# Two value projections as seven quarter products each, with a quarter of both beside the preparation of x

## The chip, the core and the metric

The kernel runs on one core of a Trainium2 chip. Its engines work side by side, each through its own list of instructions in a fixed order: TensorE (PE: matrix products and transposes), VectorE (DVE), ScalarE (ACT), GpSimd (POOL) and SyncE (SP), which here issues nearly all transfers (DMAs) between HBM and the on-chip memory SBUF. TensorE writes into banks of PSUM, from which ACT and DVE read. An instruction that waits holds back all behind it on its engine. The metric is device time in microseconds; lower is better.

## The reference

One layer of a streaming encoder: an input projection, two attentions, two output projections. The change touches the input projection.

```python
def project(x, norm_w, w_in, q_norm_w, k_norm_w):
    h = rms_norm(x, norm_w) @ w_in
    sb_q, sb_k, sb_v, sb_z, cb_q, cb_k, cb_v, cb_z, g_sb, g_cb = jnp.split(h, SPLIT_POINTS, axis=-1)
    ...
```

x has 1024 prompt rows and 64 sample rows of 1024 elements; w_in has 6144 columns in float32. The values of the two branches are the 512 columns from 1024 (sb_v) and the 512 from 3072 (cb_v). cb_k and cb_q (from 2560 and 2048) are normalised per head. The values go out as results and are used by the attentions.

## The kernel before, in words

**Precision.** Every float32 operand is split into a high and a low half (a rounded copy, made by ACT, and the rest, made by a subtraction on DVE or POOL). A product is three matmuls: high by high, low by high, high by low. `whi`/`wlo` and `whix`/`wlox` are the halves of weights with 512 of the 1024 inner rows and 256 columns; x stands as `xa`, `xm`, `xb` (high and low halves of its two inner halves) with 1088 columns, one per token; `xs` holds the 64 sample rows, high beside low.

**First stage (L279 to L315, loop at L543).** Each of nine tiles of x (128 rows; the sample is tile 8) is squared and summed on ACT, its inverse root made on POOL, scaled on DVE (`xn`), turned by eight transposes into two PSUM tiles `pt`, and copied out by ACT and DVE. Beside this runs the first of six *natural* blocks of 256 columns: per token tile 24 matmuls of 128x256 (16 for the sample), 208 in a block. The blocks are sb_v's first half, cb_k, cb_k, cb_q, cb_q, sb_v's second half. A tile's result is in one of three PSUM banks (`acc`). For values, ACT copies it to `vst` (three buffers), which SP stores twice (L334 to L336). For q and k, `evac_nat` squares it on ACT, multiplies and sums on DVE, roots on POOL; `norm_nat` scales on ACT one tile later; `post_nat`, up to three tiles later, turns it through the one PSUM buffer `pk` and copies the halves to `hl`, which is stored for the attention.

**Sums.** `make_t` gives sixteen jobs: sums of x's four quarters (inner half by token half), t0 to t3, 544 columns each. A job is three additions on DVE (L189), a rounded copy on ACT (`t2h`, `t3h`, L172) and a rest on DVE (`t2l`, `t3l`, L173), put one job later. Half of the jobs run in the natural blocks (t0, t1); the eight for t2 and t3 begin at the fifth tile of the last block, into space that the work on q and k has left.

**Quarter products (L670 to L735).** cb_v is made by a scheme that needs seven products of quarters in place of eight: x quarters, their sums t0 to t3, and sums of weight quarters, combined by additions out of PSUM. Each has 48 matmuls (L706) with 256 weight columns; there are seven, with 32 sample matmuls (L656). Their weights are split by `split_quad` (L476 ACT, L478 POOL or DVE: eight splits, six on POOL). Then the next stage (L870) makes the remaining columns by the same scheme, using x, t0 to t3 and raw weights loaded by `load_raw`.

**What sets the order.** The program is written out in the order in which each engine performs it; there is no scheduler. SP performs loads and stores in the order of the code, and a load into a buffer waits until its last reader is done. On POOL there are only roots, splits and a few copies.

## Time and profile before

| | us |
|---|---|
| median of 3 runs | 958.56 (957.79 to 960.04) |
| the profiled execution | 960.42 |
| its span, first to last instruction | 958.6 |
| TensorE busy | 949.6 |
| DVE busy | 586.1 |
| ACT busy | 498.1 |
| POOL busy | 394.2 |
| first product (L530) starts | 9.65 |
| second natural block starts | 41.67 |
| first sample matmul of cb_v (L656) starts | 174.05 |
| next stage (L870) starts | 216.38 |

A row of a timeline is start, duration, engine, line, operation, output<-input, shape and count, and in brackets the engine's idle time before it and what ended that. Matmuls overlap: 0.28 us is one's latency, and the distance of starts is its pace. A row of DMAs gives the line's count, the size and the median time from issue to landing.

### The profile page before, as it was taken

The page shows a single profiled execution, that of the slowest core. Times are in us where ns is not written, and L with a number is a line of the kernel's source. Part 1 is how long each engine was busy: PE and PEld are TensorE (multiplying, and loading weights), DVE is VectorE, ACT ScalarE, POOL GpSimd, SP SyncE. Part 2 cuts the span into 40 slices and gives each one's busy share as a digit, 9 for nine tenths or more (in the row PEclk, how much of TensorE's full clock was granted, in tenths as well). Part 3 has the DMA queues.
Part 4 walks back from the last instruction along what each step waited for, and adds up shares of the span by engine and source line. Part 5 has one row for each costly group of instructions (what it writes and reads, how often), then busy time and mean ns, then how long its engine had stood idle before and what let it go on. Part 6 is the DMA issues. An engine that isn't in the chain of part 4 may idle for free.

```text
span 958.6 us, 20550 instructions
## 1 busy us (share of the span) xinstructions
PE 949.6 (99%) x7595; PEld 902.7 (94%) x7595; DVE 586.1 (61%) x1156; ACT 498.1 (52%) x1159; POOL 394.2 (41%) x393
## 2 busy tenths in 40 slices
PE   9999999999999999999999999999999999999998
PEld 8999999999999999999999988888888888999998
DVE  6656675974445555533322389777777775499735
ACT  6557774323434433333332476767886873466220
POOL 3276664244444666555532100111430012676641
PEclk9999999999999999999999999999999999999999
DMA  7747757145656555565424997768899933852742
GB/s 228 248 138 239 262 203 236 40 127 165 192 176 194 164 176 167 160 183 179 143 86 121 279 251 193 192 192 235 247 285 248 246 91 120 252 168 71 225 140 73
DMA packets 173497, 175.77 MB, mean 183 GB/s; under 512 B 30921, under 2 KB 157645, under 8 KB 173270
## 3 DMA queue, kind: packets, MB, share of 16 engines
...
## 4 chain that ended last, share of the span: by engine, by line
PE 92%; DVE 3%; ACT 2%; DMA 1%; POOL 1%; issue 1%; ACTq 0%; DVEq 0%
PE b L870 29%; PE acc L530 15%; PE o L1392 7%; PE z L1295 7%; PE pt L1348 7%; PE b L1717 6%; PE acc L1146 5%; PE acc L1039 5%; PE b L1188 4%; PE b L706 4%; PE pk L372 1%; PE pt L303 1%; DMA wraw<-in_w_in_dram 1%; DVE acc L1233 1%; PE acc L1760 1%
## 5 line engine op out<-in xcount | busy, mean ns | idle before, releaser
L1348 PE MATMUL pt<-ident,be 128*128 128x128 f32 (+1 forms) x568 | 87.1, 277 | 0.9 <-ACT wT L1357 0.6
L1295 PE MATMUL z<-ks,sq 128*128 128x320 f32 (+5 forms) x384 | 87.7, 338 | 0.0
L1317 DVE TENSOR_TENSOR_SCAN be<-be,imp 128x128 f32<-128x128 f32 (+7 forms) x64 | 82.8, 1342 | 8.1 <-ACT be L1298 8.0
L1357 ACT ACTIVATE wT<-pt 128x512 f32<-128x512 f32 (+3 forms) x123 | 57.2, 499 | 44.2 <-PE pt L1348 44.1
L1348 PEld LDWEIGHTS pt<-ident,be 128*128 128x128 f32 (+1 forms) x568 | 66.2, 140 | 13.7 <-issue 5.3
L870 PE MATMUL b<-xm,wlox 128*128 128x256 f32 (+1 forms) x336 | 76.0, 286 | 0.0
L878 DVE TENSOR_TENSOR u<-b,s 128x256 f32<-128x256 f32 (+1 forms) x56 | 24.3, 440 | 77.1 <-PE b L870 70.0
L1295 PEld LDWEIGHTS z<-ks,sq 128*128 128x128 f32 x384 | 63.5, 190 | 2.2 <-ACT be L1298 0.9
L1392 PE MATMUL o<-wT,vp 128*64 128x256 f32 (+1 forms) x608 | 64.1, 356 | 0.0
L1392 PEld LDWEIGHTS o<-wT,vp 128*64 128x64 f32 x608 | 40.3, 136 | 22.4 <-issue 5.4
L870 PEld LDWEIGHTS b<-xm,wlox 128*128 128x128 f32 x336 | 56.8, 188 | 0.0
L1320 ACT ACTIVATE be<-be,sm 128x640 f32<-128x640 f32 (+5 forms) x68 | 47.2, 694 | 17.7 <-DVE sm L1319 17.5
L530 PE MATMUL acc<-whi,xa 128*128 128x256 f32 x192 | 52.6, 294 | 0.0
...
L459 POOL TENSOR_TENSOR whix<-ws,whix 128x512 fp32r<-128x512 f32 x28 | 36.6, 1307 | 33.2 <-ACT whix L458 25.8
L1298 ACT ACTIVATE be<-z 128x384 f32<-128x384 f32 (+6 forms) x104 | 48.2, 521 | 3.1 <-PE z L1295 2.6
L530 PE MATMUL acc<-whi,xm 128*128 128x256 f32 x192 | 49.7, 278 | 0.0
L530 PE MATMUL acc<-wlo,xa 128*128 128x256 f32 x192 | 49.6, 278 | 0.0
L530 PE MATMUL acc<-whix,xb 128*128 128x256 f32 x192 | 49.6, 278 | 0.0
L530 PE MATMUL acc<-whix,xm 128*128 128x256 f32 x192 | 49.6, 278 | 0.0
L530 PE MATMUL acc<-wlox,xm 128*128 128x256 f32 x192 | 49.5, 278 | 0.0
L1308 ACT ACTIVATE be<-be,sm 128x640 f32<-128x640 f32 (+5 forms) x68 | 47.3, 695 | 3.8 <-DVE sm L1300 3.3
...
## 6 DMA issues: line engine op xcount, KB each, us to landing
wraw<-in_w_in_dram SPq DMA_DIRECT2D x31, 512.0 KB, 4.5
wrawx<-in_w_in_dram SPq DMA_DIRECT2D x16, 512.0 KB, 6.0
...
xt<-in_x_prompt_dram SPq DMA_DIRECT2D x8, 512.0 KB
d_kcbT<-hl SPq DMA_DIRECT2D x8, 512.0 KB, 6.0
d_qcbT<-hl SPq DMA_DIRECT2D x8, 512.0 KB, 4.3
ks<-d_ksbT SPq DMA_DIRECT2D x16, 256.0 KB, 4.6
```

What stands on the lines that cost most here:

```text
L530: TE.matmul(ps, x, w, start=first, stop=last)
L870: TE.matmul(ps[:, :m], w[:, hl_, k], right[s](x)[:, k, a:b], start=s < 3 and k == 0 and e == 0, stop=k == 3 and e == 2, skip_group_check=s ...
L1039: TE.matmul(ps[:, :b - a], w[:, k], xk(x, k)[:, a:b], start=k == 0 and n == 0, stop=k == KT - 1 and n == 2)
L1146: TE.matmul(ps[:, :e - a], w[:, p, cw], g[:, a:e], start=m % 12 == 0, stop=m % 12 == 11)
L1295: TE.matmul(z[:, :m], s[:, e, q0:q0 + 128], ks[:, h, o + x:o + y], start=(e, h) == parts[0], stop=(e, h) == parts[-1])
L1298: A.activation(be[:r, x:y], z[:r, :m], AF.Sigmoid, scale=-0.125)
L1308: A.activation(be[:, :n], be[:, :n], AF.Exp, bias=kp[:, j:j + 1], scale=-1.0, accum_out=kp[:, 2:3])
L1317: V.tensor_tensor_scan(be[:r, n - 1::-1], be[:r, n - 1::-1], im[:, ::-1], 0.0, op0=OP.mult, op1=OP.max)
L1348: TE.transpose(pt[:kr, x, :r], be[:r, kb * 128:kb * 128 + kr], ident[:r, :r])
L1357: A.activation(w[:, sl:sl + m, q0:q0 + r], pt[:, :m, :r], AF.Copy)
L1392: TE.matmul(o[hd * 64:hd * 64 + 64, c0:c1], vv[:kr, kb, hd * 64:hd * 64 + 64], wT[b, p, j, hd, s // 4][:kr, s % 4, c0:c1] if j < 4 else wT ...
L1717: TE.matmul(ps[:, t], left[s](xs_, k)[:, ts_], wt_[:, k], start=s < 3 and t == k == e == 0, stop=k == 3 and e == 2, skip_group_check=s > 2 ...
```

## The change

Both value projections are now made by the quarter scheme. For j=0 (sb_v) and j=1 (cb_v) the first two of the products (x's two inner halves of the first 512 tokens by the weights of the first 256 columns) need no sums: they are made beside the preparation of x, in place of the first natural block. The result of the first is copied to `vst` and stored to a new HBM buffer `d_s1`; the second goes on in the same PSUM bank and gives the final values. With them go the sample's products for these columns. These are 112 matmuls for each j (L552).

Then come four natural blocks (cb_k, cb_k, cb_q, cb_q; 832 matmuls), and the remaining ten quarter products in the order ORDER (480 matmuls, L783), with 32 for the sample's other columns (L686, the entries with s=0). `load_s1` loads the stored partial results into `u2` when the first quarter product is done; the first two products of j=0 are held in PSUM until then. t2's space is opened when the last q tiles are through, t3's when `hl` is; the sums for t2 and t3 are at the eight places of TJ. All twelve splits are on POOL (L496).

The columns of x are laid out anew: each half has 512 prompt and 32 sample columns, so that the sums and the next stage's output cut at even places (four transposes fewer; `pieces`, `out`). Tiles of x are prepared in the order 0, 1, 2, 3, 8, 4, 5, 6, 7. In the listings below, line numbers of the changed kernel lie 2 to 50 higher for the same code (L552 for L530, L336 for L334, L286 for L284, L174 for L172, L494 and L496 for L476 and L478).

First place: tiles 1 and 2 in the first stage on TensorE, before (`acc_324` is tile 0, `acc_387` tile 1, `acc_447` tile 2):

```order
L530 MATMUL acc_324<-wlo_274,xa_150 128x256 x4
L303 MATMUL pt_349<-ident_138,xn_305 128x128 x4
L303 MATMUL pt_356<-ident_138,xn_305 128x128 x4
L530 MATMUL acc_324<-wlox_276,xm_151 128x256 x4
L530 MATMUL acc_387<-whi_269,xa_150 128x256 x4
L530 MATMUL acc_387<-whix_272,xm_151 128x256 x4
L530 MATMUL acc_387<-whi_269,xm_151 128x256 x4
L530 MATMUL acc_387<-whix_272,xb_152 128x256 x4
L530 MATMUL acc_387<-wlo_274,xa_150 128x256 x2
```

and now (`acc_293` is tile 0, `acc_356` tile 1):

```order
L552 MATMUL acc_293<-wlox_283,xm_153 128x256 x4
L552 MATMUL acc_356<-whi_250,xa_152 128x256 x4
L552 MATMUL acc_356<-whi_250,xm_153 128x256 x4
L552 MATMUL acc_356<-wlo_259,xa_152 128x256 x4
L552 MATMUL acc_356<-whix_281,xm_153 128x256 x4
L552 MATMUL acc_356<-whix_281,xb_154 128x256 x2
L305 MATMUL pt_378<-ident_140,xn_337 128x128 x4
L305 MATMUL pt_385<-ident_140,xn_337 128x128 x4
```

A tile's 24 matmuls were one accumulation in any order; now the twelve with `whi`, `wlo` come first and are read out between, and the twelve with `whix`, `wlox` follow in the same bank.

ACT there, before (two tiles' copies out, `vst_383` and `vst_437`):

```order
L284 ACTIVATE sq_366,ms_367<-xt_205 128x1024
L320 ACTIVATE fl_378<-acc_280 64x256
L334 ACTIVATE vst_383<-acc_324 128x256
L313 ACTIVATE xa_150<-pt_406 128x4x128
L313 ACTIVATE xm_151<-pt_413 128x4x128
L284 ACTIVATE sq_423,ms_424<-xt_278 128x1024
L334 ACTIVATE vst_437<-acc_387 128x256
```

and now:

```order
L311 ACTIVATE xm_153<-pt_324 128x4x128
L286 ACTIVATE sq_331,ms_332<-xt_203 128x1024
L286 ACTIVATE sq_340,ms_341<-xt_208 128x1024
L336 ACTIVATE vst_352<-acc_293 128x256
L336 ACTIVATE vst_369<-acc_356 128x256
L311 ACTIVATE xa_152<-pt_378 128x4x128
L311 ACTIVATE xm_153<-pt_385 128x4x128
L286 ACTIVATE sq_395,ms_396<-xt_285 64x1024
L336 ACTIVATE vst_409<-acc_356 128x256
L133 ACTIVATE whi_418<-wraw_210 128x1024
L336 ACTIVATE vst_430<-acc_413 128x256
```

Each tile's bank is now read out twice, and squares and a weight split stand between the readings.

Second place: ACT in the quarter products, before (`whi_3054` is the last split but one):

```order
L476 ACTIVATE whi_2850<-s1_2759 128x1024
L476 ACTIVATE whix_2854<-wrawx_2404 128x1024
L711 ACTIVATE s1_2892<-b10_2867 128x512
L172 ACTIVATE t3h_2650<-d_2838 128x544
L711 ACTIVATE s1_2925<-b11_2900 128x512
L172 ACTIVATE t3h_2650<-d_2894 128x544
L476 ACTIVATE whi_2933<-wraw_2562 128x1024
L476 ACTIVATE whix_2991<-wraw_2243 128x1024
L172 ACTIVATE t3h_2650<-d_2927 128x544
L172 ACTIVATE t3h_2650<-d_3020 128x544
L476 ACTIVATE whi_3054<-q11_2564 128x1024
```

and now (`whi_2763`, `whix_2843`, `whi_2912`, `whi_3006` and `whix_3067` are for q=4, 5, 6, 8 and 9):

```order
L494 ACTIVATE whi_2763<-made2_2201 128x1024
L174 ACTIVATE t2h_2652<-d_2738 128x544
L174 ACTIVATE t2h_2652<-d_2787 128x544
L494 ACTIVATE whix_2843<-made1_2200 128x1024
L174 ACTIVATE t2h_2652<-d_2837 128x544
L174 ACTIVATE t3h_2699<-d_2874 128x544
L494 ACTIVATE whi_2912<-wrawx_2767 128x1024
L174 ACTIVATE t3h_2699<-d_2906 128x544
L494 ACTIVATE whix_2950<-wraw_2664 128x1024
L174 ACTIVATE t3h_2699<-d_2944 128x544
L174 ACTIVATE t3h_2699<-d_2983 128x544
L494 ACTIVATE whi_3006<-wrawx_2916 128x1024
```

All copies of the t2 and t3 sums but one now stand among the splits from q=4 on.

Third place: SP around the start of the quarter products, before:

```order
L335 DMA d_sbv_59<-vst_2799 128x256
L336 DMA out_3_dram<-vst_2799 128x256
L335 DMA d_sbv_59<-vst_2834 128x256
L336 DMA out_3_dram<-vst_2834 128x256
L412 DMA wraw_3058<-in_w_in_dram 128x4x256
L412 DMA wraw_3060<-in_w_in_dram 128x4x256
```

and now (`hl_2569` holds the last four tiles of q, `u200` and `u201` are `u2` of j=0):

```order
L487 DMA wrawx_2597<-in_w_in_dram 128x4x256
L53 DMA d_qcbT2_68<-hl_2569 256x1x512
L53 DMA d_qcbT3_69<-hl_2569 256x1x512
L487 DMA wraw_2664<-in_w_in_dram 128x4x256
L707 DMA u200_2707<-d_s10_126 128x512
L707 DMA u201_2708<-d_s10_126 128x512
```

Before, these were the stores of the last value block, with q stored earlier; now the last stores of q stand here, and the loads of the partial results behind them.

The diff, cut to its core:

```diff
-XO = 576
+XO = HF
+SW = 576
...
+    d_s1 = [dram.tile([128, 1024], F32, name=f"d_s1{j}") for j in range(2)]
...
-        NB = [1024, 2560, 2816, 2048, 2304, 1280]
-        NV = 3072
+        QO = [0, 1, 2, 3, 8, 4, 5, 6, 7]
+        NB = [1024, 3072, 2560, 2816, 2048, 2304]
...
+        def evac_v(i, t, ps, n):
+
+            if t == 8:
+                put_s(i, 0, fold(p0.tile([64, 256], F32, name="fl", bufs=1), ps))
+                return
+            v = p0.tile([128, 256], F32, name="vst", bufs=3)
+            A.activation(v, ps, AF.Copy)
+            if n == 0:
+                SP.dma_start(d_s1[i][:, 256 * t:256 * t + 256], v)
+                return
+            SP.dma_start(VD[i][0][128 * t:128 * t + 128, 0:256], v)
+            if i == 0:
+                SP.dma_start(o_sbv_p[128 * t:128 * t + 128, 0:256], v)
...
+        def early(at):
+            if at in READY:
+                ready(READY.index(at) + 1)
+            elif at == 52:
+                W.split((1, 0))
+            elif at == 88:
+                W.split((1, 1))
+                load_nat(2, 1)
+            elif at == 70:
+                SP.dma_start(wqk[:, 0], q_norm_w[0:1, :].to_broadcast([128, 64]))
+                SP.dma_start(wqk[:, 1], k_norm_w[0:1, :].to_broadcast([128, 64]))
+            elif at == 140:
+                load_rb()
+            elif at == 160:
+                W.split((2, 0))
+                load_nat(3, 0)
+            elif at == 196:
+                W.split((2, 1), V)
+                load_nat(3, 1)
+
...
+        READY = [20, 42, 62, 82, 106, 130, 154, 178]
+        at, opened, got = 0, {}, []
+        for i, todo in enumerate(([(t, n) for t in range(4) for n in (0, 1)] + [(8, 2)],
+                                  [(0, 0), (1, 0), (0, 1), (2, 0), (1, 1), (3, 0), (2, 1), (8, 2), (3, 1)])):
+            for t, h in todo:
+                if h != 1:
+                    opened[t] = (psA if len(got) % 3 == 2 else psF).tile([128, 512], F32, name="acc")[:, :256]
+                    got.append(t)
+                ps = opened[t]
+                if t == 8:
+                    steps = [(k, n) for n in range(2) for k in range(KT)]
+                else:
+                    steps = [(4 * h + k, n) for n in range(3) for k in range(4)]
+                for m, (k, n) in enumerate(steps):
+                    early(at)
+                    at += 1
+                    product(ps, t, 2 if t == 8 else 3, k, n, m == 0 and h != 1, m == len(steps) - 1)
+                evac_v(i, t, ps, h)
...
-                        W.split((i + 1, h), V if i == 0 and h else None)
-                    if i + 2 < nb:
-                        load_nat(i + 2, h)
-                    elif i + 2 == nb:
-                        load_quad(h, 0, *((natx, "wrawx", 1) if h else (wpool, "wraw", 2)))
-                if (i, ti) == (0, 4):
-                    load_rb()
+                        W.split((i + 1, h))
+                        if i + 2 < nb:
+                            load_nat(i + 2, h)
+                        elif h == 0:
+                            load_quad(0, 1, 1)
+                        else:
+                            load_quad(0, 0, 1)
+                            load_quad(0, 0, 0, True)
+                    elif h == 0:
+                        split_quad(made[2])
+                        load_quad(0, 1, 0, True)
+                        load_quad(1, 1, 1)
+                    else:
+                        split_quad(made[1])
...
+                if (i, ti) == (nb - 1, 1):
+                    for n in (1, 2):
+                        made[n] = pn.tile([128, 4, 256], F32, name=f"made{n}", bufs=1)
+                    sum_w(1, quad[0, 0, 1], quad[0, 1, 1], OP.add)
+                if (i, ti) == (nb - 1, 2):
+                    sum_w(2, made[1], quad[0, 0, 0], OP.subtract)
...
+        LEFT = {1: sum_of(1), 2: sum_of(0), 6: half_of(1, 1), 4: sum_of(2), 5: sum_of(3)}
+        ORDER = [(0, 1), (0, 2), (0, 6), (0, 0), (1, 1), (1, 2), (1, 6), (1, 0), (0, 4), (0, 5), (1, 4), (1, 5)]
+        SPLIT = {(0, 1): (0, 1, 0), (1, 0): (0, 0, 1), (2, 1): 2, (4, 0): 1, (5, 0): (1, 1, 0), (5, 2): (1, 0, 1),
+                 (6, 1): (0, 0, 0), (8, 0): (0, 1, 1), (9, 0): (1, 0, 0), (10, 0): (1, 1, 1)}
+        LOAD = {(0, 1): [(1, 0, 0, True)], (1, 0): [(1, 0, 1)], (2, 1): [(1, 1, 0, True), (0, 0, 1)],
+                (5, 0): [(0, 0, 0, True)], (5, 2): [(1, 0, 0)], (6, 0): [(1, 0, 1)], (6, 1): [(0, 1, 1, True)],
+                (8, 0): [(1, 1, 1, True)]}
+        TJ = [(1, 1), (2, 0), (2, 2), (4, 0), (4, 2), (5, 0), (5, 2), (6, 0)]
+        BANKS = {0: "2", 2: "1", 4: "3", 5: "2", 6: "1", 8: "3", 10: "2"}
+        u, bank, held = {}, {}, []
+
+        def load_s1(j, pool):
+            for x in "23":
+                u[j, x] = [pool.tile([128, 512], F32, name=f"u{x}{j}{c}", bufs=1) for c in range(2)]
+            for c in range(2):
+                SP.dma_start(u[j, "2"][c], d_s1[j][:, 512 * c:512 * c + 512])
+
+        def evac_p(j, s, c, ps):
+            if s < 3:
+                d = u[j, "23"[s - 1]][c]
+                V.tensor_tensor(out=d, in0=ps, in1=u[j, "2"][c], op=OP.add)
+                return
+            v = nu.tile([128, 512], F32, name="o")
+            V.tensor_tensor(out=v, in0=ps, in1=u[j, "2" if s == 5 else "3"][c], op=OP.add)
+            put_v(j, 0 if s == 6 else 1, 0 if s == 5 else 1, c, v)
...
+        for q, (j, s) in enumerate(ORDER):
             if s == 0:
+                sample(j, 0, comb[3 + 4 * j])
+                continue
+            wh, wl = comb[q]
             for c in range(2):
                 for tt in range(2):
+                    at = q, 2 * c + tt
+                    if q == 0:
+                        if at == (0, 0):
+                            norm_nat(*raw1)
+                            pend.append(raw1[:3])
+                            sum_w((0, 1, 0), quad[0, 1, 0], made[2], OP.subtract)
+                        post_nat(*pend.pop(0))
+                    elif at == (1, 0):
+                        assert not pend
+                        p1x.close()
+                        open_t((2,))
+                        pst.close()
+                        psB = sx.enter_context(tc.tile_pool(name="a2p", bufs=1, space=PS))
+                    elif at == (1, 2):
+                        p1hx.close()
+                        open_t((3,))
+                        nu = ph.enter_context(tc.tile_pool(name="nu", bufs=2))
+                        nux = ExitStack()
+                        load_s1(0, nux.enter_context(tc.tile_pool(name="nua", bufs=1)))
+                    elif at == (2, 1):
+                        sum_w(1, quad[1, 0, 1], quad[1, 1, 1], OP.add)
+                        sum_w(2, made[1], quad[1, 0, 0], OP.subtract)
+                    elif at == (4, 0):
+                        load_s1(1, nu)
+                    elif at == (4, 1):
+                        sum_w((1, 1, 0), quad[1, 1, 0], made[2], OP.subtract)
+                    elif at == (6, 0):
+                        sum_w((0, 0, 0), quad[0, 0, 0], quad[0, 0, 1], OP.subtract)
+                    elif at == (8, 0):
+                        sum_w((1, 0, 0), quad[1, 0, 0], quad[1, 0, 1], OP.subtract)
+                    elif at == (10, 0):
+                        nux.close()
+                    elif at == (10, 2):
+                        prep(0)
+                    elif at == (11, 0):
+                        ws = sx.enter_context(tc.tile_pool(name="ws", bufs=3, side="right"))
+                        presum(1)
+                        prep(1)
+                    if at in TJ:
+                        next(tjobs)
+                    if at == (2, 0):
+                        for e in held:
+                            evac_p(*e)
+                    if at in SPLIT:
+                        n = SPLIT[at]
+                        split_quad((made if isinstance(n, int) else quad)[n])
+                    for e in LOAD.get(at, ()):
+                        load_quad(*e)
+                    if at == (9, 0):
+                        load_raw(0)
+                        load_raw(1)
+                    elif at == (10, 0):
+                        load_raw(2)
+                    if tt == 0 and s != 5:
+                        bank[c] = psF.tile([128, 512], F32, name="acc") if q == 1 else bank_of(BANKS[q], c)
+                    o = bank[c][:, 256 * tt:256 * tt + 256]
                     for k in range(4):
                         for e, (xe, w) in enumerate(((0, wh), (1, wh), (0, wl))):
+                            TE.matmul(o, LEFT[s](xe, k, 2 * c + tt), w[:, k], start=s != 5 and k == e == tt == 0,
                                       stop=k == 3 and e == 2, skip_group_check=True)
+                if q < 2:
+                    held.append((j, s, c, bank[c]))
+                else:
+                    evac_p(j, s, c, bank[c])
+            if s == 5:
+                sample(j, 1, comb[q])
         assert not list(tjobs)
```

328 lines of the change are left out of this document (105 added, 223 removed).

## The prediction

> **What bounds the kernel now.** I read the page first (busy shares, chain), then TensorE's waits, then the timelines of the first 44 us and of 155 to 216 us, where the change works.
>
> ```profile
> span 958.6 us, 20550 instructions
> PE 949.6 (99%) x7595; PEld 902.7 (94%) x7595; DVE 586.1 (61%) x1156; ACT 498.1 (52%) x1159; POOL 394.2 (41%) x393
> PE 92%; DVE 3%; ACT 2%; DMA 1%; POOL 1%; issue 1%; ACTq 0%; DVEq 0%
> ```
> ```profile
> PE pc L486 <- POOL half L257: 1.4, 1, 1.4
> ...
> PE acc L656 <- POOL wlo L478: 0.3, 1, 0.3
> ```
>
> TensorE is busy for 99% of the span and makes up 92% of the chain of waits; of the rows of what TensorE waited for (total, times, longest), the first is its longest wait and the last the only one between 155 and 216 us. So two things count: how many matmuls there are, and every wait that the new order puts before one.
>
> **Fewer matmuls.** The pace, from TensorE's timeline (start, duration), 16 matmuls apart:
>
> ```profile
> 41.67 0.28 PE L530 MATMUL acc<-whi,xs 128*128 128x256 f32 x1
> ...
> 43.48 0.28 PE L530 MATMUL acc<-whi,xa 128*128 128x256 f32 x1
> ```
>
> That is 1.81/16 = 0.113 us each. Before there are 6x208 natural products, 336 of quarters and 32 of samples: 1616. After there are 224 early ones, 4x208, 480 and 32: 1568. The 48 fewer are worth 5.4 us. Output transposes fall from 44 to 40; eight took 0.79 us (first and last row here), so 0.4. The 0.3 us wait above goes too. Gain: 6.1 us, all on the path. It is the only gain.
>
> **The early products (the 224 beside x's preparation).** They end before at 43.48 (16 of them lie in the second block). TensorE, ACT and POOL there:
>
> ```profile
> 9.65 1.03 PE L530 MATMUL acc<-whi,xs 128*128 128x256 f32 x4
> 25.64 1.04 PE L303 MATMUL pt<-ident,xn 128*128 128x128 f32 x8
> 26.43 0.48 PE L530 MATMUL acc<-whi,xm 128*128 128x256 f32 x2
> ```
> ```profile
> 10.01 1.05 ACT L131 ACTIVATE whix<-wrawx 128x1024 fp32r<-128x1024 f32 x1
> 11.64 0.60 ACT L313 ACTIVATE xm<-pt 128x512 fp32r<-128x512 f32 x1
> 12.12 1.06 ACT L284 ACTIVATE sq<-xt 128x1024 f32<-128x1024 f32 x1
> 13.30 1.06 ACT L284 ACTIVATE sq<-xt 128x1024 f32<-128x1024 f32 x1
> 18.52 0.38 ACT L334 ACTIVATE vst<-acc 128x256 f32<-128x256 f32 x1
> ```
>
> Without a stall: 9.65 + 224x0.113 + eight groups of transposes at 0.79 = 41.3, so before stalls some 2 us here. After, each tile's second product (t,1) goes on in the bank of its first, and its first matmul waits until ACT has copied (t,0) out. TensorE has 12 matmuls (1.36 us) of cover, and ACT works through other things first. For tile 1 these are two copies of x (0.5 each from row to row), two squares (1.15 each with their read-back), the copy of (0,1) and the copy of (1,0) (0.38 each): 4.1 us from about 13.2, so 17.3, where TensorE has finished (1,0) at 15.6: 1.7 us. The same count gives 0.65 for tile 0 (whix stands ahead), 1.65 for tile 2 (the whole split of the next weights, 1.05, stands ahead), 1.7 for tile 3, 0.6 for the sample; and the three vst buffers, each held by a store (4.1 to landing, in the fence below), add up to 1.65 at tile 2. With 0.5 for the first wlox, now on POOL, this is 8.5. The first product comes at 9.85 (its x copy waits behind a second square), so the end is 9.85 + 31.6 + 8.5 = 50.0: **+6.5**. Bounds: without the store wait and with one square of tile 1 out of the way, +3.7; with a store of 6.0 us, as the slowest row below, +8.4.
>
> ```profile
> wrawx<-in_w_in_dram SPq DMA_DIRECT2D x16, 512.0 KB, 6.0
> d_qcbT<-hl SPq DMA_DIRECT2D x8, 512.0 KB, 4.3
> ks<-d_ksbT SPq DMA_DIRECT2D x16, 256.0 KB, 4.6
> d_sbv<-vst SPq DMA_DIRECT2D x16, 128.0 KB, 4.1
> ```
>
> **The first quarter product (q=0).** I count from the end of the last natural product. Unstalled, the ten quarter products, 32 sample matmuls and four late transposes of q take 10x5.44 + 3.6 + 1.0 = 59.0 us. Before, the last block emptied its queue of normalised tiles early; now four of them fall between the parts of q=0. The rows of that chain:
>
> ```profile
> 131.78 1.07 ACT L354 ACTIVATE qn<-qn,rsn 128x64 f32<-128x64 f32 x4 [0.24 <-POOL rsn L275]
> ```
> ```profile
> 129.65 0.52 POOL L274 TENSOR_SCALAR rsn<-msn 128x4 f32<-128x4 f32 x1 [0.77 <-DVE msn L345]
> 130.25 1.50 POOL L275 TENSOR_TENSOR rsn<-rsn,half 128x4 f32<-128x4 f32 x1
> ```
> ```profile
> 132.79 0.41 DVE L377 TENSOR_TENSOR hl<-pk,hl 128x256 fp32r<-128x256 f32 x1
> ```
>
> The last tile's square (0.4, as the vst copy), product and sum on DVE (0.4 each), POOL's two steps (2.1, started 0.1 late), ACT's scaling (1.1), the copy of pk behind it (0.4) and DVE's rest (0.4) end near 5.3; TensorE wants the one pk buffer at 2.7: 2.6 us, and 0.9 at the tile before: **+3.6**, bounds 2.5 and 4.5. q=0 ends near 10.1.
>
> **The other quarter products.** What sets them, first as rows of before:
>
> ```profile
> 161.38 0.72 DVE L189 TENSOR_TENSOR d<-xm,xa 128x544 f32<-128x544 f32 x1
> ...
> 181.63 2.82 DVE L189 TENSOR_TENSOR d<-d,t1l 128x544 f32<-128x544 f32 x1
> ...
> 201.06 1.22 DVE L680 TENSOR_TENSOR s<-wrawx,s 128x1024 f32<-128x1024 f32 x1
> 202.53 0.67 DVE L721 TENSOR_TENSOR o<-b,s 128x512 f32<-128x512 f32 x1
> ```
> ```profile
> 181.16 2.70 POOL L478 TENSOR_TENSOR wlo<-s,whi 128x1024 fp32r<-128x1024 f32 x1 [16.05 <-ACT whi L476]
> ...
> 201.41 3.13 POOL L478 TENSOR_TENSOR wlo<-q,whi 128x1024 fp32r<-128x1024 f32 x1 [7.42 <-PE b L706]
> 204.50 2.40 POOL L478 TENSOR_TENSOR wlox<-s,whix 128x1024 fp32r<-128x1024 f32 x1
> ```
> ```profile
> L172 ACT ACTIVATE t3h<-d 128x544 fp32r<-128x544 f32 x4 | 2.6, 660 | 12.8 <-DVE d L189 12.8
> ```
> ```profile
> 174.05 0.28 PE L656 MATMUL acc<-whi,xs 128*128 128x256 f32 x1
> ```
> ```profile
> 180.00:185.00 5.00, 5.00 (x46) 5.00 (x46) 4.90 (x5) 3.03 (x5) 3.84 (x2) 1.00 0.00 0
> ```
>
> Each POOL split (2.4 us alone) makes one DVE sum beside it last 2.8 in place of 0.72: DVE loses 2.1 us to it. An addition out of PSUM (202.53) is not stretched. In the window (us, then PE, PEld, DVE) DVE already has 4.90 of 5 us. The eight sums for t2 and t3 just fit there because they began at 161.4, 13 us before the natural products ended (the sample's matmul at 174.05 follows them). Now they begin inside the quarter products, with ten splits on POOL.
>
> 1. q=4. q=1 and q=2 end at 21.0. The loads of the stored half sums (u) stand on SP behind the last two stores of q and reuse their space: issued near 15.5 (10.5 + 4.3, with issuing), landed at 20.2 (4.6). DVE then does four additions (0.68 each), two sums (1.22): 25.3; ACT's split 1.05 and POOL's 2.4: 28.9. The sample before it waits 1.05 for the second addition's bank. q=4's third matmul is ready at 23.1: stalls 1.05 + 5.7.
> 2. q=5 waits 0.45 for its own low half. q=6: ACT's order puts t3h of the first t3 sum ahead of the split of q=6's weights. DVE's queue from 25.3 to that sum: three jobs of three steps (2.25 each), two t2l (0.75), three additions, one weight sum = 11.6, and two splits' worth of 2.1: 41.1; ACT 0.66 + 1.05, POOL 2.4 and half a microsecond between: 45.5, against 40.3: 5.2.
> 3. q=8: the last t3 sum stands ahead of its split in the same way. From 41.1: three jobs, three rests, three additions, one sum = 12.3, plus two splits 4.2: 57.6; then 4.1: 61.8, against 52.5: 9.3 (and 0.7 at the sample before it, which waits for the additions).
> 4. q=9: its weights' load waits for the one buffer that the split just read, lands 4.6 to 6.0 later (wrawx and ks rows) at 66.5 to 67.9, then ACT and POOL: 2.8 by the lower. q=10 and 11 are ready.
>
> Sum **+25.2** (1.05 + 5.7 + 0.45 + 5.2 + 0.7 + 9.3 + 2.8). Bounds: if the splits cost DVE nothing, q=6 keeps 0.4 and q=8 5.5: 15.7; if additionally the u loads come with nothing ahead of them, 4 us sooner, about 9. Upwards, a 6 us landing at the two loads adds 3: 28.
>
> The later additions' stores go to SP behind these loads and nobody waits for them; the next stage's first weights are loaded at q=9 and have 15 us.
>
> **Sum.** Against the profiled run's 960.4 (the span's 958.6 and 1.8 around it): -6.1 + 6.5 + 3.6 + 25.2 = +29.2, so 989.6. That run is 1.9 above the median of 958.56; the forecast, against the median, is **987.5** when rounded, 3% slower.
>
> **Rivals.**
> A (0.58): as above. Own range 977 to 997: bounds of the early part (-3, +2), of q=0 (-1, +1) and of the loads (-6, +6).
> B (0.18): the splits fall beside additions out of PSUM or in DVE's gaps and cost it nothing; the quarters lose 15.7 or down to 9: 958.6 - 6.1 + 6.5 + 3.6 + 15.7 = 978, or down to 968 with the early bound. For it: DVE has six additions between the sums that matter. Against: the split at 181.16 struck the next sum at once.
>
> The Trainium skill, "SBUF — State Buffer", section "Who interferes with whom", says that a DVE instruction with two SBUF inputs blocks against a POOL instruction that reads SBUF, and that one with a single SBUF input does not, which is B's condition; the trace agrees on both (2.82, and 0.67 beside POOL's 3.13), and leaves open where the splits will fall.
>
> C (0.12), the other side: each engine's work of a stage fits under TensorE's, so that it runs ahead in the gaps and the in-order waits do not add up. DVE's own work in the quarters (eight jobs of four steps at 0.75 from start to start, 20 additions at 0.68, six weight sums at 1.22, 4 of the rest: 49 us) is less than 59. If only one start-up wait of 2 us is left, as before has in its early part, the time is 958.6 - 6.1 + 2 = 954.5. It decides when the first u addition starts before 16. Against: the stores that the u loads wait for cannot start before q=0 ends, and POOL's holds come on top of the 49.
> D (0.12): TensorE slows after each long stop.
>
> ```profile
> 1.37 2.08 PE L486 MATMUL pc<-ident 128*128 128x128 f32 x8 [1.37 <-POOL half L257]
> 5.87 1.46 PE L486 MATMUL pc<-ident 128*128 128x128 f32 x10
> ```
>
> The first eight matmuls of the kernel took 2.08 us, ten of the same four us later 1.46: 1.8 times the time each, for some 4 us, though the granted clock reads 1.00. If the three stops over 5 us each bring that back, each costs 2 us: 993.5. Nothing in before shows it: TensorE's longest wait is 1.4 us.
>
> The Trainium skill, "TensorE: Matmul & The Clock Gate", Part 1, has the array at half rate after an idle window of about 3.4 us; by its rule all of the stops at q=4, 6 and 8 would count.
>
> **How the numbers follow.** A measurement of this kernel can tell about 0.2% (1.9 us) from no change. Faster is most of C, 0.10; same is the rest of it, 0.02; slower A, B and D, 0.88. The range, 964 to 998, takes in A, D, and B but for its lowest end, and leaves out C and the extremes.
>
> **What would show it.** Right: TensorE's waits name ACT's vst and the low halves (POOL, line 496), stops near 6, 5 and 9 us in the quarter products, and DVE's sums (line 191) at 2.8 us beside POOL's splits; the first natural product starts near 50. Wrong: a first natural product below 46, u additions that start within 16 us of the last natural product, or quarter products in under 70 us.

## The result and the profile after

The changed kernel takes 998.72 us (median of 4 runs, 996.48 to 1000.09), the kernel before 958.17 beside it (957.28 to 960.04): a ratio of 1.0418 (1.0391 to 1.0445), slower. The forecast was 987.5, with a range of 964 to 998, so the direction was right, 29 us were forecast and 40.5 came, and the range ends 0.7 us too low. The profiled execution took 997.72 us, 37.3 more than that of before, which lay 2 us above its median; what follows accounts for these 37.3, where 29.2 were forecast.

From the page of the kernel after:

```profile
span 995.9 us, 20484 instructions
PE 958.6 (96%) x7547; PEld 908.6 (91%) x7547; DVE 604.6 (61%) x1167; ACT 499.2 (50%) x1151; POOL 413.2 (41%) x400
PE 79%; DVE 6%; DMA 5%; issue 3%; ACT 3%; POOL 2%; SPq 1%; DVEq 0%; ACTq 0%; POOLq 0%
```

TensorE's share of the chain of waits fell from 92% to 79%, although its instructions are 48 fewer. Its busy time even rose by 9 us: some matmuls became slower. What TensorE waited for (total, times, longest):

```profile
PE b L783 <- ACT whi L494: 8.4, 3, 4.8
PE acc L552 <- ACT vst L336: 6.3, 4, 2.8
PE b L783 <- POOL wlo L496: 5.2, 3, 1.9
PE pk L385 <- DVE hl L390: 5.2, 4, 2.8
PE b L783 <- DVE o L715: 2.1, 1, 2.1
```

Four of these rows were forecast (the splits' high and low halves, vst, pk). The one of `o` was not: `o` are two buffers in SBUF into which DVE adds a quarter product's result, and from which SP stores it.

**The early products.** TensorE's timeline of the kernel after: the stops before (t,1) of tiles 1, 2 and 3, two rows behind the longest of them, and the first natural product; below them is ACT's copy that the longest stop waited for:

```profile
18.91 0.74 PE L552 MATMUL acc<-whix,xm 128*128 128x256 f32 x4 [1.62 <-ACT vst L336]
...
25.73 0.50 PE L552 MATMUL acc<-whix,xm 128*128 128x256 f32 x2 [2.81 <-ACT vst L336]
...
27.22 1.06 PE L552 MATMUL acc<-whix,xb 128*128 128x256 f32 x4
28.08 1.05 PE L552 MATMUL acc<-wlox,xm 128*128 128x256 f32 x4
...
33.44 0.83 PE L552 MATMUL acc<-whix,xm 128*128 128x256 f32 x4 [1.37 <-ACT vst L336]
...
54.63 0.28 PE L552 MATMUL acc<-whi,xs 128*128 128x256 f32 x1
```
```profile
25.30 0.38 ACT L336 ACTIVATE vst<-acc 128x256 f32<-128x256 f32 x1 [1.02 <-DMA out_dram<-vst]
```

Of the 2.81 us, ACT spent 1.02 waiting for a `vst` buffer whose store had not landed (the forecast had 1.65 for this); before that it split the next weights.

Windows of the same stretch (us, then busy time of PE, PEld, DVE, ACT, POOL, the granted clock, the share of the DMA engines, GB/s):

```profile
25.00:30.00 5.00, 4.27 (x26) 4.27 (x26) 2.60 (x4) 2.89 (x6) 2.71 (x3) 0.71 0.54 175
...
35.00:40.00 5.00, 5.00 (x36) 5.00 (x36) 3.65 (x3) 2.07 (x4) 2.04 (x1) 0.76 0.33 73
```

From 27.22 to 28.08 four matmuls take 0.86 us from start to start, 0.21 us each where the pace of before is 0.113, and the granted clock reads 0.71 to 0.84 from 25 to 40: beside the stops, some 40 of the 224 products ran at half rate.

**The quarter products.** TensorE again; the first row begins where the last natural product ends, the last is the next stage's first:

```profile
165.41 0.38 PE L385 MATMUL pk<-ident,qn 128*128 128x128 f32 x2
166.73 0.44 PE L385 MATMUL pk<-ident,qn 128*128 128x128 f32 x2 [0.93 <-DVE hl L390]
171.49 0.44 PE L385 MATMUL pk<-ident,qn 128*128 128x128 f32 x2 [2.79 <-DVE hl L390]
192.31 0.58 PE L783 MATMUL b<-whi,t1h 128*128 128x256 f32 x1 [2.89 <-ACT whi L494]
194.74 0.58 PE L783 MATMUL b<-wlo,t1h 128*128 128x256 f32 x1 [1.63 <-POOL wlo L496]
210.19 0.39 PE L783 MATMUL b<-wlo,xm 128*128 128x256 f32 x1 [1.92 <-POOL wlo L496]
223.14 0.58 PE L783 MATMUL b<-whi,t2h 128*128 128x256 f32 x1 [4.80 <-ACT whi L494]
225.56 0.58 PE L783 MATMUL b<-wlo,t2h 128*128 128x256 f32 x1 [1.63 <-POOL wlo L496]
247.53 0.36 PE L783 MATMUL b<-whix,t3h 128*128 128x256 f32 x1 [2.06 <-DVE o L715]
249.22 0.58 PE L783 MATMUL b<-wlox,t3h 128*128 128x256 f32 x1 [1.21 <-POOL wlox L496]
...
257.07 0.28 PE L918 MATMUL b<-xa,wlox 128*128 128x256 f32 x1
```

q=4 stops twice (192.31, 194.74), q=6 at 210.19, q=8 twice (223.14, 225.56), q=11 twice (247.53, 249.22). Shorter waits, not shown, are 0.35 us at the sample before q=4 (188.27), 0.69 at q=6 (207.77) and 0.62 at q=9 (233.42). DVE, POOL and ACT there, and one window:

```profile
186.23 1.29 DVE L712 TENSOR_TENSOR u<-b,u 128x512 f32<-128x512 f32 x2 [3.06 <-issue]
...
207.93 2.79 DVE L191 TENSOR_TENSOR d<-d,xb 128x544 f32<-128x544 f32 x1
...
218.08 1.22 DVE L417 TENSOR_TENSOR wrawx<-wrawx,wraw 128x1024 f32<-128x1024 f32 x1
...
222.81 1.28 DVE L715 TENSOR_TENSOR o<-b,u 128x512 f32<-128x512 f32 x2
```
```profile
207.79 2.35 POOL L496 TENSOR_TENSOR wlo<-wrawx,whi 128x1024 fp32r<-128x1024 f32 x1 [7.62 <-ACT whi L494]
...
223.16 2.35 POOL L496 TENSOR_TENSOR wlo<-wrawx,whi 128x1024 fp32r<-128x1024 f32 x1 [7.58 <-ACT whi L494]
```
```profile
221.48 0.66 ACT L174 ACTIVATE t3h<-d 128x544 fp32r<-128x544 f32 x1 [3.87 <-DVE d L191]
222.05 1.04 ACT L494 ACTIVATE whi<-wrawx 128x1024 fp32r<-128x1024 f32 x1
```
```profile
195.00:200.00 5.00, 5.00 (x33) 5.00 (x34) 4.93 (x6) 1.60 (x2) 2.27 (x1) 0.72 0.89 278
```

The weights for q=8 are summed by 219.3 (218.08, 1.22), but ACT splits them only at 222.05, behind t3h, which waited for DVE's sum: the order of ACT, as forecast. DVE is busy 4.93 of 5 us in that window, while the clock is at 0.72, and POOL's split at 207.79 stretched the sum at 207.93 from 0.72 to 2.79.

**Where the time went**, by the starts of stages (us; "by count" is what the number of matmuls and transposes alone would change, at the pace of before):

| stretch | before | after | by count | lost | forecast |
|---|---|---|---|---|---|
| up to the end of the 224 early products | 43.48 | 54.63 | 0 | +11.2 | +6.5 |
| natural blocks | 130.57 | 110.78 | -22.8 | +3.0 | 0 |
| quarter products and samples | 42.33 | 91.66 | +17.3 | +32.0 | +28.8 |
| next stage starts | 216.38 | 257.07 | -5.4 | +46.1 | +35.3 |

The next stage starts 40.7 us later and the span grows by 37.3; the later stages give back 3.4, of which 1.2 are a wait (for kf, L789) that is gone and 0.4 fewer transposes; the rest is unexplained.

### The profile page after: what moved, and what is told of

The parts are those of the page before. It is cut to its first block, busy times and chain, and to the rows that moved or that the text cites. A ratio compares the mean times of both kernels' runs of the same rounds, so it can differ in the third digit from the quotient of the medians.

```text
span 995.9 us, 20484 instructions
## 1 busy us (share of the span) xinstructions
PE 958.6 (96%) x7547; PEld 908.6 (91%) x7547; DVE 604.6 (61%) x1167; ACT 499.2 (50%) x1151; POOL 413.2 (41%) x400
## 3 DMA queue, kind: packets, MB, share of 16 engines
q1 hardware_dynamic: 168534, 166.92, 56.5%
## 4 chain that ended last, share of the span: by engine, by line
PE 79%; DVE 6%; DMA 5%; issue 3%; ACT 3%; POOL 2%; SPq 1%; DVEq 0%; ACTq 0%; POOLq 0%
PE b L918 29%; PE b L1765 8%; PE acc L552 7%; PE o L1440 7%; PE z L1343 7%; PE pt L1396 6%; PE b L1236 5%; PE acc L1194 5%; DVE d L191 3%; PE acc L1087 2%; PE b L783 1%; DMA d_csbT<-hc 1%; SPq L53 1%; POOL wlox L496 1%; POOL rsn L277 1%
## 5 line engine op out<-in xcount | busy, mean ns | idle before, releaser
L1343 PE MATMUL z<-ks,sq 128*128 128x320 f32 (+5 forms) x384 | 87.7, 338 | 0.0
L1440 PEld LDWEIGHTS o<-wT,vp 128*64 128x64 f32 x608 | 40.3, 137 | 22.3 <-issue 5.3
L1368 ACT ACTIVATE be<-be,sm 128x640 f32<-128x640 f32 (+5 forms) x68 | 47.2, 694 | 17.7 <-DVE sm L1367 17.6
L991 POOL DMA_DIRECT2D d_osb<-zt x20 | 10.8, 541 | 102.1 <-DVE zt L1454 43.8
L476 POOL TENSOR_TENSOR whix<-ws,whix 128x512 fp32r<-128x512 f32 x28 | 37.0, 1321 | 38.6 <-ACT whix L475 37.0
L552 PE MATMUL acc<-whix,xm 128*128 128x256 f32 x160 | 41.5, 283 | 6.3 <-ACT vst L336 6.3
L1236 PE MATMUL b<-og,whi 128*128 128x384 f32 (+1 forms) x192 | 46.7, 327 | 0.0
L820 ACT ACTIVATE hl<-u 128x256 f32<-128x256 f32 (+1 forms) x40 | 16.9, 432 | 56.4 <-issue 16.4
L476 POOL TENSOR_TENSOR wlo<-ws,wlo 128x512 fp32r<-128x512 f32 x28 | 39.3, 1402 | 14.2 <-ACT wlo L475 13.7
L918 PE MATMUL b<-t0h,whix 128*128 128x256 f32 (+1 forms) x224 | 44.6, 289 | 0.0
L918 PE MATMUL b<-t3h,whi 128*128 128x256 f32 (+1 forms) x224 | 44.6, 289 | 0.0
```

What stands on the lines that cost most here:

```text
L476: G.tensor_tensor(out=t[:, 1], in0=src, in1=t[:, 0].bitcast(F32), op=OP.subtract)
L552: TE.matmul(ps, x, w, start=first, stop=last, skip_group_check=i < 2)
L918: TE.matmul(ps[:, :m], w[:, hl_, k], right[s](x)[:, k, a:b], start=s < 3 and k == 0 and e == 0, stop=k == 3 and e == 2, skip_group_check=s ...
L1236: TE.matmul(pp[uu][:, :n], w[:, p, uu * 128:uu * 128 + 128], g[:, a:e], start=p == 0 and m == 0, stop=p == NPAIR - 1 and m == 2)
L1343: TE.matmul(z[:, :m], s[:, e, q0:q0 + 128], ks[:, h, o + x:o + y], start=(e, h) == parts[0], stop=(e, h) == parts[-1])
L1440: TE.matmul(o[hd * 64:hd * 64 + 64, c0:c1], vv[:kr, kb, hd * 64:hd * 64 + 64], wT[b, p, j, hd, s // 4][:kr, s % 4, c0:c1] if j < 4 else wT ...
```

## The experiments

Each experiment is an edit of the changed kernel, timed in three rounds; the kernel before took 958.25 to 958.82 us beside them. Ratios are to it; the changed kernel's own is 1.0418 (1.0391 to 1.0445). A quarter phase's length runs from the last natural product's end to the next stage's first matmul (91.66 in the changed kernel).

**Half rate: idle products in the stops.** Products of the identity into a spare bank stand ahead of the (t,1) products and of q=4, 6, 8 and 10, so that TensorE is busy while it would wait.

```diff
+                if i == 0 and h == 1 and t:
+                    for m in range((0, 12, 22, 12)[t]):
+                        TE.matmul(spare[:, m % 4 * 128:m % 4 * 128 + 128], ident, ident, start=True, stop=True)
...
+        KEEP = {4: (22, 12), 6: (5, 15), 8: (38, 12), 10: (16, 8)}
```

> The changed kernel, with idle products (identity by identity, into a bank that is not yet in use) put where TensorE stopped: 12, 22 and 12 before the second products of tiles 1, 2 and 3 beside x's preparation, and 34, 20, 50 and 24 around the first products of q=4, 6, 8 and 10; nothing is left out. Theory 1 (the stops come from waits on ACT, POOL and DVE, and TensorE runs at half rate for some microseconds after each long one): the granted clock stays at 1.00 between 25 and 40 us and in the quarter products, the 224 early products end near 50 in place of 54.6, q=4 and q=8 get their weights' low halves as late as before, and the time is about 991 (4.5 from the early part, 3 to 4 from the quarters). Rival (the slow stretches come from something beside TensorE, as POOL's splits or the transfers): the stretches stay at 0.21 us a matmul, and the time stays at 998.7 or grows by what the idle products take.

Measured: 1001.70 (1001.27 to 1002.46), 1.0456 (1.0441 to 1.0472). The granted clock is 0.997 over the span, against 0.986, but the fillers were too many: a filler takes twice what was reckoned, as TensorE's timeline of this run shows:

```profile
23.04 5.07 PE L590 MATMUL b<-ident 128*128 128x128 f32 x44
```

22 of them (recorded as 44 instructions) took 4.8 us, 0.22 each, and outlasted the 2.8 us stop. The run says little on the price of the half rate, so it was repeated with fewer.

```diff
+                    for m in range((0, 6, 11, 6)[t]):
...
+        KEEP = {4: (12, 5), 6: (6, 7), 8: (27, 6), 11: (8, 4)}
```

> As the run with idle products before it, where one of them took 0.23 us in place of the 0.11 it was given, so that they outlasted the stops; now half as many: 6, 11 and 6 beside x's preparation, 17, 13, 33 and 12 around the first products of q=4, 6, 8 and 11. Theory 1 (after a stop TensorE runs at half rate, and that is part of the loss): the granted clock is 1.00 throughout, the 224 early products end at 50 to 51 in place of 54.6, the low halves of q=4 and q=8 come as late as before, what follows q=8 and q=11 is 4 shorter, and the time is about 990. Rival (the half rate fills time that would be waited anyway): the clock is 1.00, but the time stays at 997 or more.

Measured: 996.14 (993.95 to 1000.0), 1.0403 (1.0373 to 1.0432). The stretch of stops and the window behind them in this run, to be held against 2.81 us and 0.71 above:

```profile
25.98 0.51 PE L552 MATMUL acc<-whix,xm 128*128 128x256 f32 x2 [0.42 <-ACT vst L336]
```
```profile
25.00:30.00 5.00, 4.58 (x40) 4.23 (x38) 2.41 (x4) 2.78 (x6) 2.52 (x3) 1.00 0.56 179
```

The clock stays at 1.00 in the early part, whose products end at 52.18, 2.5 us sooner; the quarter phase takes 90.3, only 1.4 less. There the clock is 0.50 in two short stretches only (170.4 to 173.7, behind q=0's stop, and 231.9 to 235.1), and POOL starts q=8's low half 57.4 us after the last natural product, as late as before (57.8). So the half rate is real, but most of it in the quarters seems to fill time that TensorE would wait anyway: at full rate it arrives sooner and waits longer. The time lies between the theory's 990 and the rival's 997, and does not stand out from that of the changed kernel.

**The early stops.** First, DVE copies the first block's (t,0) out in ACT's place:

```diff
-            A.activation(v, ps, AF.Copy)
+            if n == 0 and i == 0:
+                V.tensor_copy(v, ps)
+            else:
+                A.activation(v, ps, AF.Copy)
```

> The changed kernel, with the copies of the first partial results of sb_v (tiles 0 to 3) on DVE in place of ACT; nothing else differs. Theory 1 (TensorE stops beside x's preparation because that copy stands on ACT behind squares and a split): the stops of 1.6, 2.8 and 1.4 us fall to 0.5 each or less, the clock stays at 1.00 there, the 224 products end at 47 to 48 in place of 54.6, and the time is 991 to 992. Rival (the preparation of x itself sets the pace of this part): the stops move to the transposes or to x's copies and the end stays above 52; 997 to 999.

Measured: 1000.96 (999.45 to 1002.37), 1.0447 (1.0428 to 1.0466): no gain, and the expectation fell. TensorE's longest wait, and DVE just before it (line numbers are 3 higher there):

```profile
14.98 0.71 PE L555 MATMUL acc<-whix,xm 128*128 128x256 f32 x4 [3.24 <-DVE vst L337]
```
```profile
11.01 3.49 DVE L295 SCALAR_TENSOR_TENSOR xn<-xt,rs,nw 128x512 f32<-128x512 f32 x2
14.43 0.41 DVE L337 COPY vst<-acc 128x256 f32<-128x256 f32 x1
```

DVE is in order as well, and there the copy stands behind the scaling of x, whose two instructions took 3.49 us beside a POOL split (1.41 for the next tile). The other stops, of 2.21, 1.11 and 2.00, stand in the same places, and the early products end at 57.87. The stop only changed its engine. Second, (t,1) gets a bank of its own, out of five that are free there, and DVE adds (t,0) when it reads it:

```diff
+            v = p0.tile([128, 256], F32, name="vst", bufs=4)
             if n == 0:
+                A.activation(v, ps, AF.Copy)
+                part[i, t] = v
...
+            V.tensor_tensor(out=v, in0=ps, in1=part.pop((i, t)), op=OP.add)
...
+        ring = [(psF, "acc"), (psA, "acc"), (psQ, "b20"), (psF, "acc"), (psQ, "b21")]
```

> The changed kernel, with each early product in a PSUM bank of its own (the two banks of the quarter products are free then): the second product of a tile no longer goes on in the first one's bank, and DVE adds the two in place of ACT's second copy. Theory 1 (TensorE stops because the second product waits for ACT's copy of the first): these stops vanish, the clock stays at 1.00, the 224 products end at 45 to 46 in place of 54.6, and the time is 989 to 990. Rival (ACT's and DVE's whole work beside x's preparation is more than TensorE's there): the stops move to the transposes or to the banks, the end stays at 51 or later, 995 or more.

Measured: 990.64 (989.24 to 991.24), 1.0343 (1.0323 to 1.0363), close to the 989 to 990 that the theory had. The longest waits left in the early part, and the window of the half rate:

```profile
14.41 0.66 PE L305 MATMUL pt<-ident,xn 128*128 128x128 f32 x4 [1.50 <-DVE xn L295]
18.60 1.29 PE L305 MATMUL pt<-ident,xn 128*128 128x128 f32 x8 [1.01 <-DVE xn L295]
```
```profile
25.00:30.00 5.00, 4.36 (x38) 3.95 (x37) 4.79 (x9) 3.21 (x8) 2.65 (x6) 1.00 0.79 261
```

No wait for vst, full clock, and the early products end at 47.29, 7.3 us sooner; the quarter phase stays at 91.7. So reading a bank between two products of one accumulation costs up to 7.3 of the 11.2 us, with the half rate that it brings. The run also gives `vst` a fourth buffer and takes ACT's second copies away, and does not tell the three apart. The rest is waits for the preparation of x, which the stops had covered (3.1 with two short ones), and a slightly slower pace.

**What holds the quarter products.** The sums for t2 and t3 are cut short: one addition in place of three, which leaves their low parts out.

```diff
-            for op, v in rest:
+            for op, v in rest[:1 if n > 1 else 3]:
```

> The changed kernel, with two of the three additions of each t2 and t3 sum left out (16 DVE instructions less; the columns made from t2 and t3 are then not the reference's). Theory 1 (DVE's queue, with POOL's holds, sets when q=6 and q=8 get their weights): both stops shrink to under 1 us, the low halves come about 4 us sooner at q=6 and 10 us at q=8, and the time is near 987. Rival (the loads of the weights or POOL's splits by themselves set it): the low halves come at the same places within 2 us and the time stays above 995.

Measured: 991.96 (989.9 to 992.94), 1.0350 (1.0328 to 1.0372). The quarter phase takes 83.8, 7.9 less. q=6 does not stop, and q=8 only at its low half, which comes 51.6 us after the last natural product in place of 60.2:

```profile
219.76 0.38 PE L783 MATMUL b<-wlo,t2h 128*128 128x256 f32 x1 [1.75 <-POOL wlo L496]
```

DVE's sums do set q=6 and q=8; the time fell by 6.8 us, not by the 12 expected. Next, POOL's low halves of the splits go to DVE, from those for q=4 on:

```diff
-                        split_quad((made if isinstance(n, int) else quad)[n])
+                        split_quad((made if isinstance(n, int) else quad)[n], V if q >= 2 else None)
```

> The changed kernel, with the low halves of the quarter products' weights from q=4 on made by DVE in place of POOL; nothing else differs. Theory 1 (DVE's own queue is the bound; a hold by POOL costs it 2.1 and a split of its own 1.2 and up to 1.05 for ACT's half): no sum lasts 2.8 any more, the low halves come 1 to 2 sooner at each of q=4, 6 and 8, and the time is 995 to 998. Rival (POOL's holds are most of what DVE loses): 990 or less.

Measured: 993.55 (991.67 to 994.29), 1.0368 (1.0349 to 1.0388), between the two theories: faster than the first had it, slower than the rival's 990. Work was added to the engine that sets the end, and the phase shrank to 87.7. DVE's timeline of this run, and ACT's high half for q=8:

```profile
209.55 1.22 DVE L496 TENSOR_TENSOR wlo<-wrawx,whi 128x1024 fp32r<-128x1024 f32 x1
...
212.04 0.72 DVE L191 TENSOR_TENSOR d<-d,xb 128x544 f32<-128x544 f32 x1
```
```profile
219.78 1.04 ACT L494 ACTIVATE whi<-wrawx 128x1024 fp32r<-128x1024 f32 x1
```

A split costs DVE 1.14 to the next start and is done 1.1 us sooner than POOL's 2.35; from q=4 on no sum is stretched by the 2.1 that a POOL split took. The shorter split alone would explain part of the gain, so the two are told apart at q=8, counted from the last natural product (165.67 here, 165.41 in the changed kernel): ACT starts its high half at 54.1 in place of 56.6, and the low half reaches TensorE at 56.5 in place of 60.2. Of these 3.7 us, 2.5 are DVE's shorter queue, and the rest is the shorter split. At q=6 the low half did not come sooner, as was expected (45.2 in place of 44.8). Then only the order is changed: q=6's split stands ahead of the t3 sum on ACT.

```diff
-                 (6, 1): (0, 0, 0), (8, 0): (0, 1, 1), (9, 0): (1, 0, 0), (10, 0): (1, 1, 1)}
+                 (6, 0): (0, 0, 0), (8, 0): (0, 1, 1), (9, 0): (1, 0, 0), (10, 0): (1, 1, 1)}
...
-                    if at in TJ:
+                    if at in TJ and at not in SPLIT:
                         next(tjobs)
...
                         split_quad((made if isinstance(n, int) else quad)[n])
+                        if at in TJ:
+                            next(tjobs)
```

> The changed kernel, with the splits of the weights of q=6 and q=8 written ahead of the copies of the t3 sums on ACT; nothing else differs. Theory 1 (the splits wait behind t3's copies, which wait for DVE's queue): q=6's low half comes at 207 in place of 210.2 and no longer stops TensorE, q=8's at 222.7 in place of 225.6; 995 to 996 in all, since q=8 decides. Rival (the weights' sums or their loads are what is late, not the place on ACT): both come as late as before, 998.7.

Measured: 996.28 (991.06 to 999.12), 1.0393 (1.0357 to 1.0428); not to be told from the changed kernel. q=6's stop is gone, as expected, but the phase takes 91.2: q=8's stop at its high half is 6.09 where it was 4.80. There ACT no longer waits for t3h but for DVE's sum of the weights, which starts 54.8 us after the natural products (52.7 in the changed kernel): with the order changed, DVE's queue itself is what is late. In the profiled run half rate at q=0 delayed the first u additions by 1.5 us (22.3 us after the natural products, against 20.8 in the changed kernel), and q=8's low half still came 0.5 sooner (2.9 were expected); by these numbers what the order brings is some 2 us at most. Last, in addition a t2 sum is moved ahead into q=0, and the results of s=4 and 5 go to free buffers, not to `o`:

```diff
-        TJ = [(1, 1), (2, 0), (2, 2), (4, 0), (4, 2), (5, 0), (5, 2), (6, 0)]
+        TJ = [(0, 3), (1, 1), (2, 2), (4, 0), (4, 2), (5, 0), (5, 2), (6, 0)]
...
-            v = nu.tile([128, 512], F32, name="o")
+            if s in (4, 5):
+                v = made[s - 3][:, 2 * c:2 * c + 2].rearrange("p k n -> p (k n)")
+            else:
+                v = nu.tile([128, 512], F32, name="o")
```

> The run with the splits ahead of t3's copies, and two changes more: the first two t2 sums start earlier (beside q=0 and at the start of q=1, while DVE is mostly idle), and the results of the t2 and t3 products leave through space of their own, so that no addition waits for a store. Theory 1 (DVE's queue sets q=8): q=8's low half comes 3 to 4 sooner than with the splits ahead alone (225.1), q=11 stops 2 less, 990 to 991. Rival (the loads of the partial results, not DVE's queue, set everything after them): q=8's low half comes at 224 to 225 again, and only the 2 of q=11 are gained: 994.

Measured: 992.09 (990.92 to 993.14), 1.0356 (1.0338 to 1.0374); the phase takes 84.7. q=8's low half starts 59.05 us after the natural products, 0.6 before that of the last run, where 3 to 4 were expected. Moving the sum brought nothing: DVE starts the first two t2 sums 10.6 and 14.9 us after the natural products, as in the changed kernel. q=11 no longer stops, and nearly all of the gain lies behind q=8 (25.6 us from its low half to the next stage in place of 31.6). The two `o` buffers, of which each is held until its stores have landed, were worth about 6 us, with both stops of q=11 and the half rate behind them.

**Where the chain of the quarters starts.** The forecast let the loads of u wait for the last two stores of q. These stores now go out with the first four tiles (the last half of q then holds other tokens' values):

```diff
-                    rdma(dst[p0 + j][:, :, (t - 3) * 128:(t + 1) * 128], h[:, j, :, 0:512])
+                    if t == 3 or i < nb - 1:
+                        rdma(dst[p0 + j][:, :, (t - 3) * 128:(t + 1) * 128], h[:, j, :, 0:512])
+                    if t == 3 and i == nb - 1:
+                        rdma(dst[p0 + j][:, :, 512:1024], h[:, j, :, 0:512])
```

> The changed kernel, with the last two stores of q left out behind the last tiles and two others of the same size, from the tiles before, issued earlier in the last natural block (half of q's last block then holds other tokens' values, not the reference's). The loads of the partial results then find no store ahead of them on SP, nor one that still reads the space they are loaded into. Theory 1 (those stores are why DVE's additions start 20.8 us after the last natural product): they start near 16, the stop at q=4 shrinks from 4.5 us to 1 to 2, q=8's low half comes 3 to 4 sooner than 60.2 after the last natural product, and the time is 994 to 995. Rival (DVE's own queue behind the additions is so long that their start does not matter, or the loads wait for something else): the additions start at 20 to 21 again, or q=8 comes no sooner; 998 to 999.

Measured: 998.29 (996.37 to 1002.99), 1.0421 (1.0392 to 1.0449): no difference. SP's queue of this run, and DVE's (the natural products end at 168.3):

```profile
178.69 0.39 SPq L490 DMA_DIRECT2D wrawx<-in_w_in_dram  x1
181.97 0.39 SPq L490 DMA_DIRECT2D wraw<-in_w_in_dram  x1
182.58 0.81 SPq L710 DMA_DIRECT2D u<-d_s  x2
```
```profile
178.54 0.42 DVE L390 TENSOR_TENSOR hl<-pk,hl 128x256 fp32r<-128x256 f32 x1 [1.21 <-ACT hl L389]
...
179.63 2.88 DVE L191 TENSOR_TENSOR d<-d,xb 128x544 f32<-128x544 f32 x1
...
187.74 1.29 DVE L715 TENSOR_TENSOR u<-b,u 128x512 f32<-128x512 f32 x2 [1.67 <-issue]
```

The loads go out 14.3 us after the natural products in place of 17.7, but the additions begin only 1.4 sooner (19.4 for 20.8), and so does q=8's low half. SP is in order, and the loads stand right behind a load of weights that itself waits for its buffer, which POOL's split frees; and DVE comes off q's last tile and two t2 sums just then, so at most 1.67 us more are to be had. So three things stand close together here: the stores, the split that frees the weights' buffer, and DVE's own work. The same start was tried from the other end, by taking two normalised tiles of q out of q=0 and into the last natural block:

```diff
+                    if m == 12 and i == nb - 1 and ti in (6, 7):
+                        post_nat(*pend.pop(0))
...
-                        post_nat(*pend.pop(0))
+                        if at[1] in (0, 3):
+                            post_nat(*pend.pop(0))
```

> The changed kernel, with two of the four late transposes of q moved back into the last natural block, so that q=0 holds two, not four; nothing else differs. Theory 1: q=0's stops of 3.7 us fall to 1 to 2, the last stores of q and with them the additions start 2 to 3 sooner counted from the last natural product, q=8's low half follows by about as much, and the time is 995 to 996. Rival (the last tile's chain through POOL sets this end wherever the other transposes stand): the additions start at 20 to 21 again and the time is 997 to 999.

Measured: 1001.39 (996.06 to 1003.32), 1.0437 (1.0405 to 1.0469). q=0's 2.79 us stop became 1.22, but the block before got stops of 1.53 and 2.37 for the same tiles, and the additions begin 19.4 us after its end, 1.4 sooner where 2 to 3 were expected; the phase stays at 91.7. No gain: the four steps from a tile's product to its transposes are some 5 us long wherever they stand.

**Together.** First the edits shown above for the bank of its own, q=6's split, the moved sum with the free buffers, and q=0's tiles; then, with them, also the low halves on DVE:

> The changed kernel with own banks for the early products, the splits ahead of t3's copies, the first two t2 sums earlier, the last results leaving through space of their own, and two late transposes of q moved back. Theory 1 (each cause stands by itself: 8.1 from the banks, 6.6 from the three edits of the quarters, 2 to 3 from the transposes): 980 to 982, still over 2% above the kernel before, with q=8 the largest stop. Rival (the parts hide one another): 985 or more.

> As the run with all of these, and the low halves from q=4 on made by DVE in place of POOL. Theory 1 (a split on DVE costs its queue no more than POOL's hold, and each low half comes a microsecond sooner; 5.2 by itself): 976 to 978, since part of it is the same wait that the earlier sums shorten. Rival (with the sums earlier, DVE is busy through the whole phase and the splits on it now cost): 981 or more.

Measured: 986.76 (986.35 to 987.17), 1.0293 (1.0278 to 1.0309), and 981.04 (980.18 to 982.31), 1.0238 (1.0221 to 1.0255). Both gain less than the sum of their parts, and both times lie where the rivals had them. But the second rival's reason does not hold: the splits on DVE brought 5.7 us here, no less than the 5.2 alone. q=8 in the first and in the second:

```profile
217.49 0.58 PE L793 MATMUL b<-whi,t2h 128*128 128x256 f32 x1 [6.11 <-ACT whi L496]
```
```profile
213.06 0.58 PE L793 MATMUL b<-whi,t2h 128*128 128x256 f32 x1 [3.62 <-ACT whi L496]
```

The second is the best version that was found, and 2.4% slower than the kernel before.

## Why the prediction came out as it did

**Direction and most of the mechanism: right.** The two places, the engines behind the waits and the order of the queues were as forecast, but for `o` and the pace of TensorE (below). Counted from the last natural product's end (165.41), forecast and measured: u additions 20.2 and 20.8, q=4's low half 28.9 and 29.3, q=6's 45.5 and 44.8, q=8's 61.8 and 60.2; the stops of q=0 sum to 3.6 and 3.7. The 48 fewer matmuls count for 5.4 us at the pace of before. By the start of the next stage 10.8 us more were lost than forecast: 4.6 in the early part, 3.0 in the natural blocks and 3.2 in the quarters; the later stages gave 3.4 back.

**The failed step: the early part's sum, +6.5.** Its stalls were forecast at 8.5 us and came to 8.1, by the distances of starts in TensorE's timeline. What the sum left out is the pace: it set 0.113 us for each of the 224 products, and some 40 of them took 0.21 after the 2.81 us stop, +3.7 by the same timeline. Some 1.2 more are slower first products behind the other stops and the transposes; before has such too, and the sum for after left them out. The upper bound of +8.4 had no term for either, and 11.2 came. The prediction knew the half rate as rival D, but only behind stops of over 5 us and in the quarters, and as something in place of A: neither A's sum nor the top of the range has both. That full rate gives back 2.5 here (the second run with idle products) is measured, and so is 7.3 for the run with banks of their own.

**Second, "q=10 and 11 are ready".** q=11 waits 2.06 for the additions of q=10, which wait for `o`'s two buffers, and 1.21 for its low half. The stops after q=0 were forecast at 25.2 in sum. They are 17.8 by the rows; the phase lost 32.0, of which q=0 has 3.7, so the other 10.5 are half rate and pace. The two add up to 28.3, near 25.2 and q=11's 3.3. That agrees with DVE's queue setting the end, so that a slow TensorE only arrives later (full rate gained 1.4 us in the second run with idle products). The nearness of 32.0 to the forecast's 28.8 is in part luck, since the parts were not those of the sum. Sized too high in the sum were the stops of q=4 (4.5 for 5.7), q=6 (2.6 for 5.2), q=8 (6.4 for 9.3) and q=9 (0.6 for 2.8).

**Third, the natural blocks at nothing.** They lost 3.0: two waits for pk (0.35 and 1.10), and a pace of 0.118 us in stretches. This stays unexplained beyond the two waits.

**A reason that held in size only.** "The stores that the u loads wait for" are one of three things that end together; taking them away moved the additions by 1.4 us, not by the 4 of the lower bound.

**The rivals.** B fell: of the ten POOL splits in the quarters five struck a t2 or t3 sum (2.78 to 2.89 us) and a sixth a weight sum (2.58 for 1.22), and with the splits from q=4 on made by DVE the phase is 4.0 us shorter. Additions out of PSUM were not stretched (1.28 for two, beside POOL's split at 223.16). The Trainium skill, "SBUF — State Buffer", section "Who interferes with whom", has the same pairs; the numbers agree. C fell at its own point: the additions started at 20.8, not before 16. D came true beside A, not in its place, and earlier than priced: in the first stage too, and with less net cost in the quarters (1.4 us came back where most of it was taken away, against three times 2), where DVE's queue sets q=8.
